# Weight low parts, convolution output and residual sums moved from POOL to DVE in a three-layer transformer kernel

## Chip, cores and metric

One core of one Trainium2 chip runs the whole program in one launch. The time is the device time in microseconds, the median of several runs. The core's engines are named as the profile names them: PE (TensorE, matrix products), PEld (its weight loads), DVE (VectorE), ACT (ScalarE), POOL (GpSimd), SP (SyncE, which issues the weight loads). Each engine works through its own instructions in order; work on different engines is ordered by semaphores alone. PEclk is the granted clock of TensorE, 1.00 for 2.4 GHz and 0.50 for 1.2 GHz.

## What is computed

512 tokens of 1024 features go through three layers, in float32.

```python
def hybrid_layer(x, c, positions, ...):             # layer 1
    ada = jax.nn.silu(c) @ w_ada + b_ada            # shift, scale and gate rows
    h = rms_norm(x, norm1_g) * (1 + scale1) + shift1
    proj = h @ w_in
    conv_out = bg * short_conv(cg * xc, conv_w)
    attn_out = dsa_attention(q, k, v, qi, ki, wi)   # 128 keys per query by an indexer
    mix = jnp.concatenate([conv_out, attn_out], axis=-1) @ w_out
    x = x + gate1 * mix
    h2 = rms_norm(x, norm2_g) * (1 + scale2) + shift2
    return x + gate2 * moe(h2, ...)                 # 64 experts, 8 a token, and a shared one

def expert_block(e, toks, gs):                      # in moe
    xb = t[toks]
    return ((silu(xb @ w1[e]) * (xb @ w3[e])) @ w2[e]) * gs[:, None]
```

Layers 2 and 3 are an attention with compressed keys (MLA) and a differential attention, each with a feed-forward block of width 2816 and layer norms. Their residual sums are `ALPHA * h + ...`.

## The kernel before

Every product is formed from two parts of its operands. An operand x is split into a high part of at most 12 significant bits (ACT, L217, `wh` for a weight tile) and the low part x minus high (a subtraction, L218, `wl`), and TensorE forms low x high, high x low and high x high (L225 to L227). `split` is the helper for all of them, so L217 and L218 stand for weights, transposed tokens (`xet`), transposed activations (`aet`) and others alike; the names tell them apart.

Weights come through `_Stream`: a list of tiles of up to 1 MB (128 partitions by 2048), loaded on SP's queue (L112) some tiles ahead into raw slots (`wraw`), then split. `get()` hands out a tile and, before that, emits the splits up to `ahead` tiles further on (`LA` = 2 in the experts). All raw tiles, high parts, low parts, transposed tokens and expert outputs (`eo`) share one pool of 22 slots of 8 KB per partition, the heap; a slot is written again only when its last reader is through, and where the reader is a transfer, when that has landed. Each tile of the list has a kind: `None` (not split), `True` (the low part is formed on DVE), or `"pool"` (the low part is formed on POOL). POOL has the convolution columns and output projection of layer 1 (`plan_attn`, `plan_sq`), the shared expert, the first two expert units and the w2 tile of all experts but the last (`plan_moe`), part of the MLA weights (`plan_mla`), some feed-forward tiles (`plan_ffn`) and most of the differential attention's input weights (`plan_diff`). POOL also forms the low part of the convolution output (`mixc`, L798), part of the residual sums of the attention half (`add` in `attn_block`, L846), and the adaptive rows (L657). It issues 51 gathers (L1213) and 67 scatters (L1218).

The expert half sorts tokens into slot blocks by expert. A unit of work is one of: 2 units of fixed experts, 25 single experts of one block, 3 experts of two blocks, and 16 pairs (two experts whose 64 rows each share a block). The order on each engine is that in which the program emits its work. For a single expert u it is:

- `get` of w1, which also emits the split of w2 of the unit before; products of w1 (`up`); `acts()` for the unit before: silu on ACT, times the w3 product on DVE (`sg`, L1395), transposes on TensorE (L230), their split (`aet`);
- `get` of w3, which emits the split of the next w1; products of w3; transposes of the next unit's gathered tokens (`xg`) and their split (`xet`, two pieces); the gather of a later block on POOL;
- `get` of w2 of the unit before, which emits the split of the next w3; its products (`down`), scaled to `eo` by DVE for the first half of the columns (L1414) and by ACT for the other (L1412); the scatter-add of `eo` to the sum `acc` in memory on POOL; the mask `P` of a later block (L1152) on DVE.

Where the slot tables of up to eight blocks are finished (a cut), DVE runs some ten small operations (L1134 to L1202), `gt` (L1140) among them. In the router, DVE finds the top 8 of 64 scores and packs the gates. In a pair, the two experts' products and down products alternate.

```python
kind = "pool" if i < 2 else True
j += [(weight("w1", 8, r), kind), (weight("w3", 8, r), kind)]
...
j.append((weight("w2", 2, r), "pool" if i < len(ops) - 4 else True))
```

Of the kernel before, what the change touches and what calls it, by code (L numbers as in the profile page):

```python
# [33 lines left out]
# slots of an expert by its rank: those below the first number have the second  # L34
# [36 lines left out]
class _Stream:  # L71
    """Weights in the order of use: loads run ahead on the SP queue, and each tile is split into two
    parts of at most 12 significant bits, whose sum is the float32 value, before it is used."""
# [41 lines left out]
    def _split(self):  # L115
        i = self.ns
        kind = self.jobs[i][1]
        if kind:
            t, n, v = self.rawt.pop(i)
            H, L = self.k.slot(F32R, "wh"), self.k.slot(F32R, "wl")  # L120
            self.k.split(H[:, :n], L[:, :n], t[:, :n], eng=self.k.nc.gpsimd if kind == "pool" else None)
            self.hl[i] = (H, L, n, v)
        self.ns += 1
# [7 lines left out]
    def more(self):  # L131
        """prepare one more tile than `ahead` asks for"""
        if self.ns < len(self.jobs):
            if self.ns not in self.rawt:
                self.pump(self.ns)
            self._split()
            self.pump(self.ns)
# [40 lines left out]
class _K:  # L178
# [35 lines left out]
    def split(self, H, L, x, scale=None, eng=None):  # L214
        nc = self.nc
        if scale is None:
            nc.scalar.activation(H, x, AF.Copy)  # L217
            (eng or nc.vector).tensor_tensor(out=L, in0=x, in1=H.bitcast(F32), op=OP.subtract)  # L218
# [13 lines left out]
    def rsqrt(self, v, n, scale, eps, name):  # L232
        """1 / sqrt(scale v + eps): a seed from the exponent, a third-order step and a Newton step, each on a
        multiple of the result that spares a product"""
# [50 lines left out]
    def proj(self, hT, nk, tiles, n=512, hook=None, w=None):  # L285
        """token-major product: weight tiles [p, kk, n] from chunk kc0 on into four PSUM tiles"""
# [33 lines left out]
    def part(self, hT, ps, tt, ws):  # L320
        """token tile tt of a product, weight tiles [(first chunk, tile)]"""
# [7 lines left out]
    def begin(self, xT):  # L329
        """the products of a block's first two weight tiles [128, 8, 256] with the first half of the tokens"""  # L330
# [16 lines left out]
    def begun(self, xT):  # L347
        """what `begin` has left of the next of its weight tiles"""
# [4 lines left out]
    def chunks(self, name, n):  # L353
        """feature-major operand in chunks of 128 features by 512 columns, as its two exact parts"""
# [39 lines left out]
    def plan_sq(self, w):  # L394
        w = w.rearrange("(k p) n -> p k n", p=128)
        return [(w[:, 4 * j:4 * j + 4, n * 512:n * 512 + 512], "pool") for j in range(2) for n in range(2)]

    def plan_attn(self):
# [3 lines left out]
        first += [(w, "pool") for w, _ in self.plan_win(2560)]  # L402
# [5 lines left out]
        j += [(cols[i:i + 2], "pool") for i in range(0, 12, 2)]  # L408
        out = self.plan_sq(self.a["w_out"][0])
        j += out[:2] + [(out[2][0], True)] + out[3:]  # L410
        return j

    def rope_p(self, t, cc, ss):
        """rotate the first 16 of each 64 columns of t [128, G, 64]; cc [128,16], ss [128,16] = [-sin | sin]"""
# [50 lines left out]
    def row(self, dst, ap, off, n):  # L465
        """one DRAM row on all partitions"""
        self.nc.scalar.dma_start(out=dst, in_=bass.AP(tensor=ap.tensor, offset=ap.offset + off, ap=[[0, 128], [1, n]]))

    def heads_T(self, dst, ps, g=None, scale=None):
        """four PSUM tiles [128 tok, 8 x 64]: (RMS norm with gain g,) partial rotation, feature-major split;  # L470
        the gain of the rotated columns goes in before the rotation, that of the others, in `scale`, after it"""
# [33 lines left out]
    def attn_block(self):  # L505
        nc, V, a, st = self.nc, self.nc.vector, self.a, self.st
        # adaptive scale and shift, and the normalised tokens, by halves of the features
# [86 lines left out]
        # remaining adaptive rows, on the scalar and Pool engines  # L594
# [68 lines left out]
        # indexer queries, keys, weights  # L663
# [43 lines left out]
        # indexer scores  # L707
# [31 lines left out]
        def topk():  # L739
            """the 128 best keys of each query, the earlier of equal ones: others get a bias of -1e30"""  # L740
# [23 lines left out]
        # values  # L764
# [5 lines left out]
        # short convolution, channel-major  # L770
# [5 lines left out]
        def conv():  # L776
            ws = []
            for c in range(4):
                w = lambda k: cw[:, k, c:c + 1]
                for i in range(3):  # L780
# [15 lines left out]
                    else:  # L796
                        V.tensor_tensor(out=y, in0=y, in1=ps, op=OP.mult)
                        self.split(*mixc(c), y, eng=nc.gpsimd)  # L798
# [8 lines left out]
        # attention  # L807
# [34 lines left out]
        def add(tt, ps, n):  # L842
# [3 lines left out]
            (V if n or last else nc.gpsimd).tensor_tensor(out=Y(tt)[:, c], in0=Y(tt)[:, c], in1=t, op=OP.add)  # L846
        last = False
        self.attend(range(HEADS), logits, value, fill(), FILL, 3)
        # the rest of the output projection and the residual, then the normalised tokens of the expert half
# [7 lines left out]
        def done(tt, *pss):  # L857
            nonlocal last
            last = tt == NT - 1
# [19 lines left out]
    def out_head(self, mix, add):  # L879
        """the first four chunks' share of an output projection; add(tt, ps, n) takes it in"""  # L880
# [22 lines left out]
    def pipeline(self, items, stages, fill=None, n=0, ready=None):  # L903
        """stages [(fn, delay)] over items; each step also emits up to n units of the background work `fill`,
        and as much of it as an item needs to be ready"""
# [24 lines left out]
    def attend(self, heads, logits, value, fill=None, n=0, bufs=3, ready=None):  # L930
        """softmax attention of `heads` in tiles of 128 queries, feature-major result"""
# [34 lines left out]
    def moe_units(self):  # L966
        """(ranks, rows of the slot blocks), in the order of work: the first FIX experts; the others by falling
        number of tokens, the busiest with two blocks, the least busy two to a block"""
# [20 lines left out]
    def plan_moe(self):  # L989
# [3 lines left out]
        j = [([wr, s1[:, :, 0:128]], "pool"), ([s1[:, :, 128:256], s3[:, :, 0:128]], "pool"),  # L993
             (s3[:, :, 128:256], "pool")]
# [13 lines left out]
        for i, (op, u, m) in enumerate(ops):  # L1008
            r = units[u][0][m]
            if op == "up":  # L1010
                kind = "pool" if i < 2 else True
                j += [(weight("w1", 8, r), kind), (weight("w3", 8, r), kind)]
                if i == 1:
                    j.append((kp(a["ws2"][0], 2), "pool"))
            else:
                j.append((weight("w2", 2, r), "pool" if i < len(ops) - 4 else True))
        return j

    def moe_begin(self, hT):
        """the router and most of the shared expert's first products, on the first half of the tokens"""  # L1020
# [66 lines left out]
    def moe_block(self, hT, h2d, x1d):  # L1087
# [20 lines left out]
        pos_b = self.const.tile([128, NT, NE], BF16, name="pos_b")  # exact up to 256, and above stays above  # L1108
# [10 lines left out]
        def pack(v, g, tmp):  # L1119
            """the gate in three exact parts"""  # L1120
# [8 lines left out]
        def tables(c, ig, is_):  # L1129
            """gather and scatter rows of n blocks from the sums c [128, n, 3] of token, tile base and one"""  # L1130
# [28 lines left out]
        def table_step(i):  # L1159
            """one block's slot list; the indices are finished for up to eight blocks at a time"""  # L1160
# [89 lines left out]
            # order of the experts  # L1250
# [40 lines left out]
            # gates  # L1291
# [31 lines left out]
        def shared():  # L1323
            """the rest of the shared expert, in steps"""
# [52 lines left out]
        # experts  # L1377
# [61 lines left out]
        def overflow():  # L1439
            """list of the blocks past the slots above"""  # L1440
# [103 lines left out]
        # blocks past the slots above  # L1544
# [63 lines left out]
    def moe_sum(self, X, acc, xT, xd):  # L1608
        """the layer's result, tile by tile: residual + gate2 * experts"""
# [536 lines left out]
```

## Time and profile before

| | us |
|---|---|
| runs | 2729.9, 2726.62, 2722.79 |
| median | 2726.62 |
| span of the profiled execution | 2724.9 |
| PE busy | 2361.5 (87%) |
| DVE busy | 1649.5 (61%) |
| ACT busy | 1056.4 (39%) |
| POOL busy | 836.8 (31%) |

The span is the stretch from the first to the last instruction that the profiler saw in one execution. A line of the page's groups gives the source line, the engine and operation, the tile written and the tiles read, their shapes, the count, the busy time, the mean of one in nanoseconds, and how long the engine sat idle just before such an instruction and what ended most of that. In the span, layer 1's attention half lies up to about 420 us, router and shared expert up to about 520, the experts up to about 1410, and layers 2 and 3 after that.

### The profile page before, as it was taken

Reading aid. Unit: us, or ns where it says so; the run is one execution under the profiler, and the core shown is the slowest. Engines: PE = TensorE matmul, PEld = TensorE weight load, DVE = VectorE, ACT = ScalarE, POOL = GpSimd, SP = SyncE. Lnnn points to the kernel's source line nnn. Section 1 sums busy time; section 2 is a strip of 40 time slices with the busy share of each in tenths; the row PEclk is TensorE's granted clock in tenths of the full one; section 3 lists DMA queues with packets and bytes.
Section 4 is the critical chain, followed back from the end, with each engine's and each line's share of the span. In section 5 each row is a group of like instructions: output and inputs, shape, how many; then the busy total and the mean of one; then the engine's idle time right before and its main releaser. Section 6 shows DMA issues by size and latency. Waiting matters only on the chain.

```text
span 2724.9 us, 33197 instructions
## 1 busy us (share of the span) xinstructions
PE 2361.5 (87%) x12964; PEld 1979.8 (73%) x12964; DVE 1649.5 (61%) x2445; ACT 1056.4 (39%) x1446; POOL 836.8 (31%) x308
## 2 busy tenths in 40 slices
PE   8778996778777887888758998999999998899998
PEld 4556765677666776777757877888888886788887
DVE  4699666577877877677656655333354666533234
ACT  2642433355545655555542532221313443222221
POOL 0653243456645655565521120000032221100001
PEclk9889998899988988898979999999999998999999
DMA  9432145588967877888861042223232122222321
GB/s 317 171 122 63 47 157 188 192 264 273 308 212 245 287 260 248 278 278 279 271 182 45 16 152 88 85 93 108 87 114 70 47 72 81 95 89 81 123 70 39
DMA packets 176593, 422.40 MB, mean 155 GB/s; under 512 B 19281, under 2 KB 97873, under 8 KB 151729
## 3 DMA queue, kind: packets, MB, share of 16 engines
q1 hardware_dynamic: 151552, 353.43, 37.8%
q0 software_dynamic: 12944, 39.20, 6.7%
q10 hardware_dynamic: 11938, 27.62, 2.8%
q8 instruction: 103, 1.69, 0.2%
q14 instruction: 56, 0.46, 0.1%
HBM read 390.78 MB, written 35.52 MB: 156 GB/s over the span
## 4 chain that ended last, share of the span: by engine, by line
PE 50%; DVE 22%; issue 9%; DMA 7%; ACT 6%; POOL 6%; ACTq 0%; POOLq 0%; DVEq 0%; SPq 0%
PE b L225 16%; PE b L226 15%; PE b L227 15%; DVE wl L218 5%; POOL wl L218 4%; ACT wh L217 4%; DMA acc<-eo,isc 3%; PE b L230 2%; DMA wraw<-in_w_dram 2%; DVE xet L218 1%; DVE gt L1140 1%; DVE work L752 1%; DVE eo L1414 1%; PE b L545 1%; POOL acc L1218 1%
## 5 line engine op out<-in xcount | busy, mean ns | idle before, releaser
L218 POOL TENSOR_TENSOR wl<-wraw,wh 128x2048 fp32r<-128x2048 f32 (+2 forms) x113 | 533.0, 4720 | 1208.6 <-ACT wh L217 1157.8
L218 DVE TENSOR_TENSOR wl<-wraw,wh 128x2048 fp32r<-128x2048 f32 x198 | 606.9, 3072 | 367.8 <-ACT wh L217 319.6
L217 ACT ACTIVATE wh<-wraw 128x2048 fp32r<-128x2048 f32 (+2 forms) x311 | 583.5, 1884 | 151.3 <-DVE wl L218 58.0
L225 PE MATMUL b<-xtl,wh 128*128 128x512 f32 (+1 forms) x928 | 342.5, 369 | 2.9 <-DVE xtl L218 2.9
L226 PE MATMUL b<-xth,wl 128*128 128x512 f32 (+1 forms) x928 | 341.0, 368 | 4.0 <-POOL wl L218 4.0
L227 PE MATMUL b<-xth,wh 128*128 128x512 f32 (+1 forms) x928 | 340.7, 367 | 0.0
L225 PE MATMUL b<-wl,xet 128*128 128x256 f32 x1072 | 319.2, 298 | 0.1
L226 PE MATMUL b<-wh,xet 128*128 128x256 f32 x1072 | 311.3, 290 | 0.8 <-DVE xet L218 0.8
L227 PE MATMUL b<-wh,xet 128*128 128x256 f32 x1072 | 310.8, 290 | 0.0
L1218 POOL DMA_INDIRECT acc<-eo,isc x67 | 102.6, 1531 | 391.9 <-DVE P L1152 121.6
L225 PEld LDWEIGHTS b<-wl,xet 128*128 128x128 f32 x1072 | 214.7, 200 | 1.7 <-ACT xet L217 0.2
L226 PEld LDWEIGHTS b<-wh,xet 128*128 128x128 f32 x1072 | 214.0, 200 | 2.4 <-DVE xet L218 0.9
L227 PEld LDWEIGHTS b<-wh,xet 128*128 128x128 f32 x1072 | 213.2, 199 | 0.0
L225 PE MATMUL b<-wl,aet 128*128 128x512 f32 x268 | 125.5, 468 | 99.6 <-POOL wl L218 99.1
L226 PEld LDWEIGHTS b<-xth,wl 128*128 128x128 f32 x928 | 175.0, 189 | 32.8 <-POOL wl L218 4.6
L225 PEld LDWEIGHTS b<-xtl,wh 128*128 128x128 f32 x928 | 175.0, 189 | 32.3 <-DVE xtl L218 3.6
L227 PEld LDWEIGHTS b<-xth,wh 128*128 128x128 f32 x928 | 174.9, 189 | 28.9
L225 PEld LDWEIGHTS b<-wl,aet 128*128 128x128 f32 x268 | 57.8, 216 | 121.2 <-POOL wl L218 108.8
L225 PE MATMUL b<-wl,ath 128*128 128x512 f32 x352 | 137.1, 390 | 0.0
L227 PE MATMUL b<-wh,ath 128*128 128x512 f32 x352 | 136.9, 389 | 0.0
L226 PE MATMUL b<-wh,atl 128*128 128x512 f32 x352 | 136.9, 389 | 0.0
L1213 POOL DMA_INDIRECT xg<-h2d,ig x51 | 124.6, 2444 | 34.3 <-issue 17.5
(463 smaller groups left out, 4649.8 us busy)
## 6 DMA issues: line engine op xcount, KB each, us to landing
wraw<-in_w_dram SPq DMA_DIRECT2D x192, 1024.0 KB
wraw<-in_ffn_w_gu_dram SPq DMA_DIRECT2D x44, 1024.0 KB
wraw<-in_w_ada_dram SPq DMA_DIRECT2D x24, 1024.0 KB
wraw<-in_ffn_w_down_dram SPq DMA_DIRECT2D x20, 1024.0 KB
wraw<-in_diff_w_in_dram SPq DMA_DIRECT2D x12, 1024.0 KB
wraw<-in_w_in_dram SPq DMA_DIRECT2D x8, 1024.0 KB
wraw<-in_w_in_dram SPq DMA_DIRECT2D x12, 512.0 KB
x<-in_x_dram SPq DMA_DIRECT2D x8, 512.0 KB
```

The costliest lines, as they stand in the source:

```text
L217: nc.scalar.activation(H, x, AF.Copy)
L218: (eng or nc.vector).tensor_tensor(out=L, in0=x, in1=H.bitcast(F32), op=OP.subtract)
L225: mm(ps, s[0], m[1], start=start, stop=False)
L226: mm(ps, s[1], m[0], start=False, stop=False)
L227: mm(ps, s[0], m[0], start=False, stop=stop)
L230: self.nc.tensor.transpose(ps, x, self.ident[:x.shape[0], :x.shape[0]])
L545: nc.tensor.matmul(ps, cb[:, kc, :], w[:, kk, :], start=False, stop=kc == 7)
L752: V.match_replace(work(qt), m8[qt - 1], work(qt), -3e38)
L1140: V.tensor_tensor(out=gt, in0=c[:, :, 2], in1=c[:, :, 1], op=OP.add)
L1213: nc.gpsimd.indirect_dma_start(out=x, out_offset=None, in_=h2d, in_offset=IndirectOffsetOnAxis(ap=idx, axis=0), bounds_check=S - 1, oob_is ...
L1218: nc.gpsimd.indirect_dma_start(out=acc, out_offset=IndirectOffsetOnAxis(ap=idx, axis=0), in_=o, in_offset=None, compute_op=OP.add)
L1414: V.tensor_scalar(o[rows, c], ps[rows], gate[rows], None, OP.mult)
```

## The change

The argument `eng` of `split` goes, and all kinds `"pool"` become `True`: 113 subtractions for weight low parts (105 of them 128 by 2048) run on DVE in their place of the program's order. So do the 4 low parts of the convolution output and the 7 residual sums. POOL keeps gathers, scatters, the adaptive rows and some fills. Comments and docstrings are left out too, so the changed program's lines have numbers up to five lower behind the changed places.

```diff
-            self.k.split(H[:, :n], L[:, :n], t[:, :n], eng=self.k.nc.gpsimd if kind == "pool" else None)
+            self.k.split(H[:, :n], L[:, :n], t[:, :n])
...
-    def split(self, H, L, x, scale=None, eng=None):
+    def split(self, H, L, x, scale=None):
...
-            (eng or nc.vector).tensor_tensor(out=L, in0=x, in1=H.bitcast(F32), op=OP.subtract)
+            nc.vector.tensor_tensor(out=L, in0=x, in1=H.bitcast(F32), op=OP.subtract)
...
-                        self.split(*mixc(c), y, eng=nc.gpsimd)
+                        self.split(*mixc(c), y)
...
-            (V if n or last else nc.gpsimd).tensor_tensor(out=Y(tt)[:, c], in0=Y(tt)[:, c], in1=t, op=OP.add)
+            V.tensor_tensor(out=Y(tt)[:, c], in0=Y(tt)[:, c], in1=t, op=OP.add)
...
-                kind = "pool" if i < 2 else True
-                j += [(weight("w1", 8, r), kind), (weight("w3", 8, r), kind)]
+                j += [(weight("w1", 8, r), True), (weight("w3", 8, r), True)]
...
-                j.append((weight("w2", 2, r), "pool" if i < len(ops) - 4 else True))
+                j.append((weight("w2", 2, r), True))
```

The other edits of this kind are in `plan_sq`, `plan_attn`, `plan_mla`, `plan_ffn` and `plan_diff`.

In a single expert's unit on DVE, before: the subtraction of w3, the scaled output, the next block's mask, then `sg`.

```order
L218 TENSOR_TENSOR wl<-wraw,wh 128x2048
L1414 TENSOR_SCALAR eo<-b,gt 128x512
L1152 TENSOR_TENSOR P<-iota_b,pos_b 128x4x64 x2
L1395 TENSOR_TENSOR sg<-sg,b 128x256
L218 TENSOR_TENSOR aet<-b,aet 128x256
L218 TENSOR_TENSOR wl<-wraw,wh 128x2048
L218 TENSOR_TENSOR xet<-b,xet 128x512 x2
L218 TENSOR_TENSOR wl<-wraw,wh 128x2048
```

The same place in the changed program:

```order
L218 TENSOR_TENSOR wl<-wraw,wh 128x2048
L1409 TENSOR_SCALAR eo<-b,gt 128x512
L1147 TENSOR_TENSOR P<-iota_b,pos_b 128x4x64 x2
L218 TENSOR_TENSOR wl<-wraw,wh 128x2048
L1390 TENSOR_TENSOR sg<-sg,b 128x256
L218 TENSOR_TENSOR aet<-b,aet 128x256
L218 TENSOR_TENSOR wl<-wraw,wh 128x2048
L218 TENSOR_TENSOR xet<-b,xet 128x512 x2
L218 TENSOR_TENSOR wl<-wraw,wh 128x2048
```

The subtraction of w2 stands between the mask `P` and `sg`; all else keeps its order.

On POOL, at the end of the first run of singles, before (`isc` holds the scatter's indices):

```order
L1218 DMA acc<-eo,isc 640x1024
L218 TENSOR_TENSOR wl<-wraw,wh 128x2048
L1213 DMA xg<-h2d,ig 64x1024
L1218 DMA acc<-eo,isc 640x1024
L218 TENSOR_TENSOR wl<-wraw,wh 128x2048
L1218 DMA acc<-eo,isc 640x1024
L1213 DMA xg<-h2d,ig 128x1024
L218 TENSOR_TENSOR wl<-wraw,wh 128x2048
L1218 DMA acc<-eo,isc 640x1024
```

and in the changed program:

```order
L1213 DMA acc<-eo,isc 640x1024
L1208 DMA xg<-h2d,ig 64x1024
L1213 DMA acc<-eo,isc 640x1024 x2
L1208 DMA xg<-h2d,ig 128x1024
L1213 DMA acc<-eo,isc 640x1024
```

A gather now follows the scatter ahead of it directly.

In the pairs on DVE, with the semaphores that each instruction waits for, before (DMASW are POOL's indirect transfers, DMAHW the loads, the others engines):

```order
L218 TENSOR_TENSOR aet<-b,aet 128x256 [waits Activation_49]
L218 TENSOR_TENSOR wl<-wraw,wh 128x2048 [waits DMAHW2_49,DVE_49,Activation_49]
L218 TENSOR_TENSOR wl<-wraw,wh 128x2048 [waits DMAHW3_49,PE_49,Activation_49]
L1414 TENSOR_SCALAR eo<-b,gt 64x512 [waits DMASW2_49,DMASW3_49,DMASW0_49,DMASW5_49,DVE_49,PE_49]
L1395 TENSOR_TENSOR sg<-sg,b 64x256 [waits Activation_49]
L218 TENSOR_TENSOR wl<-wraw,wh 128x2048 [waits DVE_49,DMAHW5_49,PE_49,Activation_49]
```

and in the changed program:

```order
L218 TENSOR_TENSOR wl<-wraw,wh 128x2048 [waits DMAHW4_49,Activation_49]
L1409 TENSOR_SCALAR eo<-b,gt 64x512 [waits PE_49]
L218 TENSOR_TENSOR wl<-wraw,wh 128x2048 [waits DMASW3_49,DMASW2_49,DMASW5_49,DMASW0_49,DMAHW5_49,DVE_49,Activation_49]
L1390 TENSOR_TENSOR sg<-sg,b 64x256 [waits Activation_49]
L218 TENSOR_TENSOR aet<-b,aet 128x256 [waits Activation_49]
L218 TENSOR_TENSOR wl<-wraw,wh 128x2048 [waits DMAHW6_49,DVE_49,Activation_49]
```

The wait for the indirect transfers, which stood at the scaled output `eo`, stands at the moved subtraction, ahead of `sg`; it is there in every second pair.

## Rows read from the trace of the kernel before

**Rows 1.** The page's costliest groups: count, busy us, mean ns of one, idle us before and releaser.
```profile
L218 POOL TENSOR_TENSOR wl<-wraw,wh 128x2048 fp32r<-128x2048 f32 (+2 forms) x113 | 533.0, 4720 | 1208.6 <-ACT wh L217 1157.8
L218 DVE TENSOR_TENSOR wl<-wraw,wh 128x2048 fp32r<-128x2048 f32 x198 | 606.9, 3072 | 367.8 <-ACT wh L217 319.6
...
L226 PE MATMUL b<-xth,wl 128*128 128x512 f32 (+1 forms) x928 | 341.0, 368 | 4.0 <-POOL wl L218 4.0
...
L225 PE MATMUL b<-wl,aet 128*128 128x512 f32 x268 | 125.5, 468 | 99.6 <-POOL wl L218 99.1
```

**Rows 2.** Timeline of DVE in one single expert: start us, duration us, operation.
```profile
894.57 2.28 DVE L218 TENSOR_TENSOR wl<-wraw,wh 128x2048 fp32r<-128x2048 f32 x1
896.77 0.74 DVE L1414 TENSOR_SCALAR eo<-b,gt 128x512 f32<-128x512 f32 x1
897.43 0.74 DVE L1152 TENSOR_TENSOR P<-iota_b,pos_b 128x256 bf16<-128x256 bf16 x2
898.10 0.41 DVE L1395 TENSOR_TENSOR sg<-sg,b 128x256 f32<-128x256 f32 x1
...
901.38 5.08 DVE L218 TENSOR_TENSOR wl<-wraw,wh 128x2048 fp32r<-128x2048 f32 x1 [1.38 <-ACT wh L217]
```

**Rows 3.** Timeline of POOL in the same expert.
```profile
899.24 5.07 POOL L218 TENSOR_TENSOR wl<-wraw,wh 128x2048 fp32r<-128x2048 f32 x1
904.47 2.94 POOL L1213 DMA_INDIRECT xg<-h2d,ig  x1 [0.16 <-issue]
```

**Rows 4.** Windows: length, busy us (count) of each engine, granted clock, DMA share, GB/s.
```profile
894.41:933.47 39.06, 31.47 (x240) 28.19 (x237) 31.70 (x28) 23.86 (x24) 26.92 (x9) 1.00 0.90 304
1087.16:1340.24 253.08, 209.04 (x1303) 187.79 (x1303) 187.77 (x111) 144.24 (x131) 146.01 (x49) 0.91 0.84 277
1198.60:1202.00 3.40, 3.14 (x7) 2.51 (x8) 3.40 (x2) 0.00 (x0) 0.21 (x1) 0.50 0.68 193
675.00:750.00 75.00, 58.71 (x434) 52.29 (x434) 62.48 (x57) 44.45 (x44) 50.40 (x19) 1.00 0.96 310
150.00:256.00 106.00, 79.18 (x345) 60.52 (x343) 101.42 (x223) 36.76 (x59) 49.85 (x26) 0.89 0.35 98
```

**Rows 5.** Timeline of PE in the same single expert; in brackets the idle time before.
```profile
898.65 0.47 PE L230 MATMUL b<-ident,sg 128*128 128x128 f32 x2 [1.07 <-DVE sg L1395]
898.88 0.36 PE L225 MATMUL b<-wl,xet 128*128 128x256 f32 x1
...
901.84 1.06 PE L230 MATMUL b<-ident,xg 128*128 128x128 f32 x8
904.36 0.50 PE L225 MATMUL b<-wl,aet 128*128 128x512 f32 x1 [1.46 <-POOL wl L218]
```

**Rows 6.** Timeline of ACT in the same expert.
```profile
902.49 1.09 ACT L217 ACTIVATE xet<-b 128x512 fp32r<-128x512 f32 x2 [1.14 <-PE b L230]
904.34 1.92 ACT L217 ACTIVATE wh<-wraw 128x2048 fp32r<-128x2048 f32 x1 [0.76 <-POOL wl L218]
```

**Rows 7.** Timeline of PE at the down products of a pair.
```profile
1198.86 0.80 PE L225 MATMUL b<-wl,aet 128*128 128x512 f32 x1 [3.03 <-POOL wl L218]
```

**Rows 8.** Timeline of DVE at a table cut.
```profile
865.67 5.33 DVE L1140 TENSOR_TENSOR gt<-tg 128x8 f32<-128x8 f32 x1
```

**Rows 9.** Timeline of PE behind that cut.
```profile
872.52 0.67 PE L230 MATMUL b<-ident,sg 128*128 128x128 f32 x2 [8.19 <-DVE sg L1395]
```

**Rows 10.** Timeline of DVE in the router, the first and the last of four.
```profile
435.64 4.67 DVE L1242 TENSOR_TENSOR ms<-ms,rb 128x256 f32<-128x256 f32 x1 [5.14 <-ACT ms L1241]
...
489.18 7.15 DVE L1152 TENSOR_TENSOR P<-iota_b,pos_b 128x512 bf16<-128x512 bf16 x4
```

**Rows 11.** Timeline of PE at the first expert unit's down products.
```profile
536.36 0.75 PE L225 MATMUL b<-wl,aet 128*128 128x512 f32 x1 [4.98 <-POOL wl L218]
```

**Rows 12.** Timeline of POOL at the table cut.
```profile
871.13 1.00 POOL L1213 DMA_INDIRECT xg<-h2d,ig  x1 [0.16 <-issue]
```

**Rows 13.** The chain that ended last, in order of time, in a pair: start, us, what.
```profile
1217.68 7.57 DMA acc<-eo,isc
```

More of the change, by code (lines that the diff above doesn't have):

```diff
@@ L395, in plan_sq @@
         w = w.rearrange("(k p) n -> p k n", p=128)
-        return [(w[:, 4 * j:4 * j + 4, n * 512:n * 512 + 512], "pool") for j in range(2) for n in range(2)]
+        return [(w[:, 4 * j:4 * j + 4, n * 512:n * 512 + 512], True) for j in range(2) for n in range(2)]
     def plan_attn(self):
@@ L401, in plan_attn @@
         first = head[1:] + self.plan_win(3584, 72) + self.plan_win(2048) + self.plan_win(1536)
-        first += [(w, "pool") for w, _ in self.plan_win(2560)]
+        first += self.plan_win(2560)
         rest = self.plan_ada([8, 9, 6, 7, 4, 5, 10, 11])
@@ L407, in plan_attn @@
         cols = [w[:, :, o + c * 128:o + c * 128 + 128] for c in range(4) for o in (0, 1024, 512)]
-        j += [(cols[i:i + 2], "pool") for i in range(0, 12, 2)]
+        j += [(cols[i:i + 2], True) for i in range(0, 12, 2)]
         out = self.plan_sq(self.a["w_out"][0])
-        j += out[:2] + [(out[2][0], True)] + out[3:]
-        return j
+        return j + out
     def rope_p(self, t, cc, ss):
@@ L845, in add @@
             V.tensor_tensor(out=t, in0=ps, in1=self.gate1[:, c], op=OP.mult)
-            (V if n or last else nc.gpsimd).tensor_tensor(out=Y(tt)[:, c], in0=Y(tt)[:, c], in1=t, op=OP.add)
-        last = False
+            V.tensor_tensor(out=Y(tt)[:, c], in0=Y(tt)[:, c], in1=t, op=OP.add)
         self.attend(range(HEADS), logits, value, fill(), FILL, 3)
@@ L857, in done @@
         def done(tt, *pss):
-            nonlocal last
-            last = tt == NT - 1
             for n in range(2):
@@ L992, in plan_moe @@
         wr, s1, s3 = kp(a["w_router"][0], 8), kp(a["ws1"][0], 8), kp(a["ws3"][0], 8)
-        j = [([wr, s1[:, :, 0:128]], "pool"), ([s1[:, :, 128:256], s3[:, :, 0:128]], "pool"),
-             (s3[:, :, 128:256], "pool")]
+        j = [([wr, s1[:, :, 0:128]], True), ([s1[:, :, 128:256], s3[:, :, 0:128]], True),
+             (s3[:, :, 128:256], True)]
         units = self.moe_units()
@@ L1010, in plan_moe @@
             if op == "up":
-                kind = "pool" if i < 2 else True
-                j += [(weight("w1", 8, r), kind), (weight("w3", 8, r), kind)]
+                j += [(weight("w1", 8, r), True), (weight("w3", 8, r), True)]
                 if i == 1:
-                    j.append((kp(a["ws2"][0], 2), "pool"))
+                    j.append((kp(a["ws2"][0], 2), True))
             else:
-                j.append((weight("w2", 2, r), "pool" if i < len(ops) - 4 else True))
+                j.append((weight("w2", 2, r), True))
         return j
@@ L1711, in plan_mla @@
             hs = slice(2 * i, 2 * i + 2)
-            j.append(([uq[:, :, hs, 0:128], uk[:, :, hs, :]], "pool"))
+            j.append(([uq[:, :, hs, 0:128], uk[:, :, hs, :]], True))
         return j + self.plan_sq(a["mla_w_o_2"][0])
@@ L1886, in plan_ffn @@
                 for o in (0, DFF):
-                    j.append((gu[:, :, o + f * 256:o + f * 256 + 256], "pool" if f == 0 else True))
+                    j.append((gu[:, :, o + f * 256:o + f * 256 + 256], True))
             for n in range(2):
                 for k in range(2 * f0, 2 * f1, 4):
-                    j.append((dn[:, k:min(k + 4, 2 * f1), n * 512:n * 512 + 512], "pool" if f0 and n else True))
+                    j.append((dn[:, k:min(k + 4, 2 * f1), n * 512:n * 512 + 512], True))
         return j
@@ L1949, in plan_diff @@
         w = self.a["diff_w_in_2"][0].rearrange("(k p) n -> p k n", p=128)
-        j = [(w[:, :, o + hp * 256:o + hp * 256 + 256], "pool" if hp or o < 2048 else True)
+        j = [(w[:, :, o + hp * 256:o + hp * 256 + 256], True)
              for hp in range(4) for o in (0, 1024, 2048)]
```

## The prediction

> **What bounds the kernel now.** I read the costliest groups first, then the timelines of the four engines over one expert, then windows by stage, then the chain of waits. TensorE is the engine to feed, and in the groups the question is who keeps it waiting: the down products (b from wl and aet) stood idle 99.6 us, 99.1 of it for POOL's low parts, while the 928 products on xth and wl, which are the projections of attention and of layers 2 and 3, stood 4.0 us for them [rows 1]. So what POOL's subtractions cost is in the expert half, and little elsewhere. The same groups show a second cost. One subtraction takes 4.72 us on POOL, and 3.07 us on DVE as a mean of 198. The timeline says why the mean is so high: the one at 894.57 took 2.28 us, with none running on POOL; the one at 901.38 took 5.08 us beside one on POOL that runs from 899.24 for 5.07 us, so to 904.31, and ended 2.15 us behind that [rows 2, 3]. DVE's subtraction stands still until POOL's is done. Over 198 of them that is 198 x (3.07 - 2.28) = 156 us of DVE time that is waiting.
>
> **A single expert.** Three of them take 39.06 us, 13.02 each, at a granted clock of 1.00 [rows 4]. TensorE has two holes in each: 1.07 us ahead of sg's transposes, for DVE, and 1.46 us ahead of the down products, for POOL [rows 5]. After the change the wait for POOL goes, but in DVE's order the w2 subtraction now stands between P and sg, and what is late next is sg. I add up the loop through it: wl 2.20 (894.57 to 896.77), eo 0.66, P 0.67, the moved wl 2.20, sg until the transposes start 0.55 (898.10 to 898.65) [rows 2, 5]; transposes 0.23, w3's products 2.96 (898.88 to 901.84), transposes of xg 0.65 until ScalarE starts on xet [rows 5, 6]; ScalarE's xet 1.09 and wh 1.92 [rows 6], and wl again. The sum is 13.1 us against 13.02 now. **Singles: nothing gained**, some 20 of them. DVE's subtraction there gets 2.8 us shorter and one of 2.2 us is put in. The two holes become one of about 2.5 us ahead of sg.
>
> **A pair** (two experts in one slot block). Ten take 253.08 us, 25.3 each, with a clock of 0.91 and a DMA share of 0.84 [rows 4]. A pair has one hole of 3.03 us for POOL's low part [rows 7], and 3.40 us at half clock behind it [rows 4]. The loop through the moved subtraction holds two of the pair's four up products more and a down product: 2.20 + 0.66 + 2.20 + 0.55 + 0.23, then four products of 2.96 (a down product is 12 matmuls of 512 columns where w3's is 24 of 256, so I take the same), 0.65 + 1.09 + 1.92 = 21.3 us. The DMA engines need no less: 0.84 x 25.3 = 21.3 us at a share of 1, and 22.1 us at the 0.96 that 675 to 750 reached [rows 4]. I take 22.1, a gain of 3.2, and 12 of the 16 pairs, since the first ones are mixed with table work: **-38 us**.
>
> **Table cuts.** Where the slot tables of up to eight blocks are finished, DVE's small gt stands 5.33 us behind POOL's subtraction [rows 8], and TensorE stands 8.19 us for sg [rows 9]. Without it gt, which has 8 columns, needs no more than sg's 0.41 [rows 2], and 2.2 us of moved wl come in: 5.33 - 0.41 - 2.2 = 2.7. Seven such places: **-19 us**. The clock behind the hole stays low, since 5 us of it are left.
>
> **Router.** Four DVE operations stand behind POOL there, from 4.67 us (ms) to 7.15 us (P, four of them) [rows 10], at about one POOL subtraction, 4.7 us [rows 1], each: -19. Four moved subtractions come into DVE's order, 4 x 2.2 = 9. **-10 us.**
>
> **First expert unit.** TensorE stands 4.98 us for a low part that is queued behind a scatter on POOL [rows 11]; on DVE it isn't behind it: **-5 us.**
>
> **Everything else.** The projections lose their 4.0 us: **-4 us.** In the indexer's top-k, 150 to 256, DVE is busy 101.4 of 106 us [rows 4]; five subtractions move there, which adds 5 x 2.2 = 11 us if DVE never stood for them on POOL, and takes off 5 x (4.7 - 2.2) = 12 if it stood for the whole of each: zero, with both as bounds. The 4 convolution and 7 residual operations lie beside TensorE work and cost nothing; uncovered they would cost 11 x 0.7 = 8. ScalarE's and SP's order doesn't change. What I cost at nothing on DVE is hidden by TensorE's products; in a single that cover is already used up.
>
> Sum: -38 - 19 - 10 - 5 - 4 = -76 on the profiled span of 2724.9, so 2648.9; the median of the runs is 1.7 above that span, which gives **2651 us**.
>
> **A rule and a row.** POOL's gather takes 2.94 us beside DVE's subtractions and 1.00 us when none runs [rows 3, 12], so each of the 118 gathers and scatters can become 1.94 us longer now that DVE subtracts more. I put nothing for it in the sum, since POOL has 533 us fewer to do [rows 1], but it lengthens the landing in rival C. The Trainium skill (SBUF — State Buffer, Who interferes with whom) says otherwise: a tensor_tensor of DVE leaves the descriptor writing of such DMAs alone, which the page marks as inferred. By the page rival C is priced at 7.57 us a wait, by the row at up to 9.5; the row decides here.
>
> **Rivals.**
> A. *DMA stays the bound in the pairs.* The DMA share there is 0.84, not 0.96, and the chain runs over a scatter that lands in 7.57 us [rows 13]: loads wait for slots, so the share can't rise. Then pairs give nothing: 2651 + 38 = **2689 us**. For it: the low clock stretch hides time in which loads caught up. Against: TensorE's hole there is ended by POOL, not by a load [rows 7].
> B. *The joined hole in the singles costs clock.* Now 1.07 and 1.46 us leave the clock at 1.00; behind 3.03 us it was at half for 3.40 us, so 1.7 us of work lost [rows 4, 5, 7]. A hole of 2.5 us lies between. If each of 20 singles pays: +34, **2685 us**.
> C. *Slower: DVE takes over POOL's waits for scatters.* A slot that a scatter reads is free only when it has landed. On POOL a subtraction stood behind that scatter in order anyway; on DVE it needs a wait of its own, and sg, aet and xet are queued behind. The order lists 19 DVE subtractions of weights with a wait for such a DMA, 11 before. If each of the 19 stands 7.57 us [rows 13]: 19 x 7.57 = 144, and 144 - 76 = +68, **2795 us**. It decides from 76 / 19 = 4.0 us each. Against: in the pairs only one of twelve subtractions has the mark, and six marked eo operations of before are one now, so of such waits on DVE there are 20 against 17. The new place is the worse one, ahead of sg.
> D. *The lock is not POOL's doing*, and DVE's subtractions stay at 3 us and more. Then 113 more on DVE are 113 x 3.07 = 347 us of it against 99 us of TensorE's waits that go; most of the 347 hides, so near no change, or slower. The rows speak against it: the end of the one follows the end of the other in the one shown [rows 2, 3].
>
> **How the numbers follow.** About 0.3%, 8 us, is what can be told from no change. The forecast has 0.55, its own range 2617 to 2682; A 0.14; B 0.15; C with D's worse part 0.11; what is left, 0.05, lies within 8 us of before. Faster: 0.55 + 0.14 + 0.15 = 0.84; same 0.05; slower 0.11. The low end takes the better bounds of each term: pairs at 21.3 (-10), the whole router (-3), singles 1 us better each (-20), the top-k's locks (-12): 2651 - 45 = 2606. The high end is A and B together, 2723, cut to 2716, since both at full price is unlikely; C lies outside.
>
> **What would show it.** Right: DVE's wl at 2.2 to 2.3 us throughout, and POOL with nothing but indirect DMAs and the adaptive rows after 400 us; gt at 0.17 us; pairs at 22 us and a DMA share near 0.96; one hole a single, ended by DVE's sg. A: pairs still at 25 us, holes ended by wh or by loads. B: singles at 14.5 us, clock under 1.00 between 675 and 750. C: DVE's wl with idle time ended by acc scatters. The prediction is wrong if singles move by more than 1 us either way, since there I claim that a 5 us wait and the 2.2 us put in its place cancel.

## Result and the profile after

The changed kernel takes 2660.0 us (median of 4 runs, 2654.9 to 2667.7) against 2728.3 before (4 runs, the three above among them): ratio 0.975, 95% interval 0.974 to 0.977. The forecast was 2651, range 2606 to 2716. The profiled execution has a span of 2660.0 us against 2724.9, so 64.9 us are to be found. Windows cut at the same instruction in both (ACT's `eo` of the second fixed expert, of the first pair and of the last unit) show where. The kernel before (length, busy time and count of PE, PEld, DVE, ACT, POOL, granted clock, DMA share, GB/s):

```profile
0.00:541.00 541.00, 433.97 (x2086) 326.50 (x2087) 379.74 (x750) 201.98 (x329) 205.06 (x106) 0.90 0.47 156
541.00:963.50 422.50, 331.29 (x2432) 299.23 (x2430) 326.94 (x342) 229.09 (x235) 251.35 (x87) 0.94 0.84 267
963.50:1407.90 444.40, 354.84 (x2226) 318.71 (x2225) 319.45 (x218) 240.69 (x222) 232.79 (x81) 0.90 0.80 260
1407.90:2724.90 1317.00, 1241.42 (x6228) 1035.36 (x6228) 623.35 (x1137) 384.64 (x660) 147.61 (x34) 0.97 0.25 83
```

and after:

```profile
0.00:526.10 526.10, 435.47 (x2087) 327.70 (x2088) 369.33 (x782) 201.82 (x330) 100.53 (x74) 0.91 0.48 161
526.10:954.00 427.90, 342.30 (x2431) 314.41 (x2429) 308.35 (x370) 226.93 (x236) 118.14 (x59) 0.91 0.87 264
954.00:1352.30 398.30, 344.29 (x2226) 318.57 (x2224) 295.70 (x249) 240.24 (x222) 110.10 (x50) 0.91 0.86 289
1352.30:2660.00 1307.70, 1235.27 (x6228) 1030.07 (x6228) 639.99 (x1171) 384.69 (x660) 1.40 (x1) 0.98 0.25 84
648.30:734.60 86.30, 69.52 (x472) 64.10 (x470) 60.54 (x57) 46.99 (x48) 27.16 (x12) 0.88 0.91 274
1077.40:1284.80 207.40, 182.46 (x1172) 170.55 (x1172) 156.56 (x118) 129.73 (x117) 58.66 (x26) 0.90 0.88 305
```

Four stages in each: up to that second unit -14.9 us, singles and table cuts +5.4, pairs -46.1, layers 2 and 3 -9.3. The last two rows of after are six singles (86.30 us, 14.4 each, clock 0.88; before 13.02 at 1.00 [rows 4]) and nine pairs (207.40 us, 23.0 each, clock 0.90; before 25.3 at 0.91 [rows 4]).

The page's groups of after:

```profile
L218 DVE TENSOR_TENSOR wl<-wraw,wh 128x2048 fp32r<-128x2048 f32 (+2 forms) x311 | 702.7, 2266 | 449.4 <-ACT wh L217 399.6
...
L226 PE MATMUL b<-xth,wl 128*128 128x512 f32 (+1 forms) x928 | 340.8, 367 | 0.0
...
L230 PE MATMUL b<-ident,sg 128*128 128x128 f32 x102 | 28.7, 377 | 132.9 <-DVE sg L1390 132.9
...
L225 PE MATMUL b<-wl,aet 128*128 128x512 f32 x268 | 113.4, 423 | 3.6 <-DVE wl L218 3.1
```

All 311 subtractions are on DVE and take 2.27 us as a mean; 198 took 3.07 and POOL's 113 took 4.72 [rows 1]. DVE's whole busy time is even lower, 1613.4 us against 1649.5, with 124 operations more. TensorE's wait for the low part of w2 fell from 99.1 us to 3.1. More than half of that came back elsewhere: the wait ahead of sg's transposes is 132.9 us, 52 more than in the kernel before:

```profile
L230 PE MATMUL b<-ident,sg 128*128 128x128 f32 x102 | 25.3, 336 | 80.9 <-DVE sg L1395 80.8
```

### The profile page after: what moved, and what is told of

It is laid out like the page before. It is cut to its first block, busy times and chain, and to the rows that moved or that the text cites. A ratio compares the mean times of both kernels' runs of the same rounds, so it can differ in the third digit from the quotient of the medians.

```text
span 2660.0 us, 32960 instructions
## 1 busy us (share of the span) xinstructions
PE 2357.3 (89%) x12964; PEld 1990.8 (75%) x12964; DVE 1613.4 (61%) x2569; ACT 1053.7 (40%) x1446; POOL 330.2 (12%) x184
## 4 chain that ended last, share of the span: by engine, by line
PE 61%; DVE 24%; ACT 8%; issue 3%; DMA 2%; POOL 1%; ACTq 0%; SPq 0%; DVEq 0%; POOLq 0%
PE b L225 19%; PE b L226 18%; PE b L227 18%; DVE wl L218 9%; ACT wh L217 4%; PE b L230 4%; ACT xet L217 2%; DVE eo L1409 1%; DVE P L1147 1%; PE b L544 1%; DVE work L751 1%; DVE m L747 1%; DMA wraw<-in_w_ada_dram 1%; DVE sg L1390 1%; DVE ln_st L1628 1%
## 5 line engine op out<-in xcount | busy, mean ns | idle before, releaser
L218 DVE TENSOR_TENSOR wl<-wraw,wh 128x2048 fp32r<-128x2048 f32 (+2 forms) x311 | 702.7, 2266 | 449.4 <-ACT wh L217 399.6
L225 PE MATMUL b<-wl,xet 128*128 128x256 f32 x1072 | 336.2, 314 | 0.1
L226 PE MATMUL b<-wh,xet 128*128 128x256 f32 x1072 | 327.0, 305 | 0.8 <-DVE xet L218 0.8
L227 PE MATMUL b<-wh,xet 128*128 128x256 f32 x1072 | 326.0, 304 | 0.0
L1213 POOL DMA_INDIRECT acc<-eo,isc x67 | 160.0, 2389 | 611.9 <-DVE P L1147 217.9
L226 PEld LDWEIGHTS b<-wh,xet 128*128 128x128 f32 x1072 | 230.9, 215 | 2.2 <-DVE xet L218 1.0
L225 PEld LDWEIGHTS b<-wl,xet 128*128 128x128 f32 x1072 | 231.0, 216 | 1.8 <-DVE wl L218 0.2
L227 PEld LDWEIGHTS b<-wh,xet 128*128 128x128 f32 x1072 | 229.8, 214 | 0.0
L230 PE MATMUL b<-ident,sg 128*128 128x128 f32 x102 | 28.7, 377 | 132.9 <-DVE sg L1390 132.9
L923 ACT ACTIVATE p<-b,nm 128x128 f32<-128x128 f32 (+3 forms) x128 | 67.1, 526 | 166.5 <-DVE nm L920 127.2
L230 PEld LDWEIGHTS b<-ident,sg 128*128 128x128 f32 x102 | 16.0, 206 | 141.9 <-issue 92.0
L225 PE MATMUL b<-wl,aet 128*128 128x512 f32 x268 | 113.4, 423 | 3.6 <-DVE wl L218 3.1
```

Of the source, the lines that this page charges most:

```text
L218: nc.vector.tensor_tensor(out=L, in0=x, in1=H.bitcast(F32), op=OP.subtract)
L225: mm(ps, s[0], m[1], start=start, stop=False)
L226: mm(ps, s[1], m[0], start=False, stop=False)
L227: mm(ps, s[0], m[0], start=False, stop=stop)
L230: self.nc.tensor.transpose(ps, x, self.ident[:x.shape[0], :x.shape[0]])
L923: nc.scalar.activation(p[:, :nk], ps[:, :nk], AF.Exp, bias=nm, accum_out=sm)
```

## Experiments

The theory: DVE's subtraction, and other DVE operations that read two operands from the local memory (`gt`, the mask `P`), stand still while POOL's subtraction runs, and the change takes that away. In the singles it gives the gain back, since w2's subtraction ahead of sg makes one long hole where two short ones were, and TensorE's clock falls behind it. Rivals: DVE was stretched by waits, not by POOL; the gain lies in other parts than w2; the singles are held by DMA.

### POOL busy with work nobody needs

Behind the scatters of each down product in the changed kernel, four subtractions of 512 columns, from a constant tile (`db`) into a spare one:

```diff
+                for _ in range(4):
+                    nc.gpsimd.tensor_tensor(out=dout.rearrange("p (a b) -> p a b", b=128), in0=db, in1=db, op=OP.subtract)
```

> The changed kernel, and behind each scatter POOL does four subtractions of 512 columns from a constant tile into a spare one; nothing reads them, so nobody waits for their result. Theory (DVE's subtraction stands still while POOL's runs): DVE's weight subtractions go up from a mean of 2.27 us to 2.6 or more, and the time by 15 to 50 us. Rival (DVE was stretched by what it waited for, not by POOL's use of memory): mean 2.27 us, time within 4 us of 2660.

Measured: 2725.5 us (10 runs), ratio to before 0.999 (0.998 to 1.001). Nothing reads what POOL writes, and 65 us are lost, more than the 15 to 50 that I wrote. The mean of DVE's 128x2048 subtractions rose from 2.295 to 2.442 us, less than I wrote: POOL's pieces let DVE in between, as the first rows show, where gt and P end while POOL's four are still running. A table cut of this run, DVE, POOL and PE in turn:

```profile
873.83 1.88 DVE L1135 TENSOR_TENSOR gt<-tg 128x8 f32<-128x8 f32 x1
...
875.83 2.45 DVE L1147 TENSOR_TENSOR P<-iota_b,pos_b 128x256 bf16<-128x256 bf16 x2
878.20 3.12 DVE L218 TENSOR_TENSOR wl<-wraw,wh 128x2048 fp32r<-128x2048 f32 x1
```

```profile
874.13 5.04 POOL L1544 TENSOR_TENSOR dout<-dum 128x512 bf16<-128x512 f32 x4
```

```profile
881.92 0.67 PE L230 MATMUL b<-ident,sg 128*128 128x128 f32 x2 [8.98 <-DVE sg L1390]
```

gt takes 1.88 us, P 2.45 and the subtraction 3.12 while POOL's four run, and TensorE's hole is 8.98 us, longer even than before the change (8.19 [rows 9]). In the changed kernel, without POOL's work, the same place reads (DVE, then PE):

```profile
854.89 0.17 DVE L1135 TENSOR_TENSOR gt<-tg 128x8 f32<-128x8 f32 x1
...
855.17 0.75 DVE L1147 TENSOR_TENSOR P<-iota_b,pos_b 128x256 bf16<-128x256 bf16 x2
855.84 2.29 DVE L218 TENSOR_TENSOR wl<-wraw,wh 128x2048 fp32r<-128x2048 f32 x1
```

```profile
858.73 0.67 PE L230 MATMUL b<-ident,sg 128*128 128x128 f32 x2 [4.76 <-DVE sg L1390]
```

The stages of the idle run, singles and cuts, then pairs (after the change 427.9 and 398.3):

```profile
525.70:983.30 457.60, 354.03 (x2434) 326.39 (x2431) 333.72 (x370) 226.79 (x235) 298.53 (x171) 0.87 0.80 248
983.30:1408.80 425.50, 345.42 (x2226) 319.35 (x2225) 331.71 (x249) 240.27 (x222) 357.30 (x182) 0.90 0.80 270
```

### POOL busy without reading

In the same place, 15 fills of a spare tile of 384 columns:

```diff
+                for _ in range(15):
+                    nc.gpsimd.memset(dout, 1.0)
```

> As the run with idle subtractions on POOL, but POOL fills a spare tile instead (15 fills of 384 columns behind each scatter, some 5 us), so it writes and reads nothing. Theory (DVE stands for POOL's reading, not for POOL being busy or for scatters and gathers being late): DVE's weight subtractions stay at a mean of 2.3 us, gt at 0.17 us, and the time within 10 us of 2660. Rival (late gathers and scatters behind POOL's work cost the time): about 2725 us as with the idle subtractions.

Measured: 2685.7 us, ratio 0.984 (0.982 to 0.986). The groups by form, DVE's subtraction and POOL's fills:

```profile
L218 DVE TENSOR_TENSOR wl<-wraw,wh 128x2048 fp32r<-128x2048 f32 x298 | 682.4, 2295 | 442.7 <-ACT wh L217 385.3 <-PE b L225 27.2 <-issue 15.6
```

```profile
L1541 POOL MEMSET dout<- 128x384 f32 x960 | 435.6, 454 | 51.6
```

The same table cut, POOL and then DVE:

```profile
853.49 7.61 POOL L1541 MEMSET dout<- 128x384 f32 x15
```

```profile
853.50 0.75 DVE L1147 TENSOR_TENSOR P<-iota_b,pos_b 128x256 bf16<-128x256 bf16 x2
854.17 2.28 DVE L218 TENSOR_TENSOR wl<-wraw,wh 128x2048 fp32r<-128x2048 f32 x1
```

POOL is as busy (436 us; the idle subtractions were 463) and DVE is not stretched: P takes 0.75 us and the subtraction 2.28 beside the fills, and the mean is 2.295 us as in the changed kernel. (gt, at 853.21, ends before the fills begin, so its 0.17 us here shows nothing.) So it is POOL's reading that holds DVE, not its being busy. But 26 us are lost all the same, where the theory claimed at most 10. Its stages (singles and cuts, pairs, the rest):

```profile
524.20:952.30 428.10, 342.49 (x2431) 314.59 (x2428) 308.36 (x370) 227.07 (x236) 307.07 (x480) 0.91 0.85 265
952.30:1361.10 408.80, 354.02 (x2226) 328.16 (x2224) 296.23 (x249) 240.15 (x222) 309.07 (x541) 0.88 0.85 281
1361.10:2682.10 1321.00, 1234.98 (x6228) 1030.65 (x6228) 640.22 (x1171) 384.52 (x660) 16.92 (x36) 0.97 0.25 83
```

Singles and cuts take what they took after the change (428.1 against 427.9 us). The pairs take 10.5 us more with a hole as long and a lower clock, and behind the experts TensorE waits up to 28.6 us for DVE's sums, 13.5 after the change: the last scatters stand behind the last fills. So reading on POOL is worth the 30 us that the run above has more in singles and cuts. In the pairs it isn't so plain. The stage read 387.1 us in `w2_only` and 404.3 in `mask_late` (both below), which have the changed kernel's order there, so 10.5 us is little more than that spread. And ten pairs without table work take 237.6 us with idle subtractions and 238.9 with fills, against 230.2 after the change and 253.0 before: what reading costs more shows in the table cuts. There the theory is at its clearest. The five units in which gt was stretched took 107.7 us before, 83.8 after the change, 108.0 with idle subtractions and 85.4 with fills.

### Which part of the change

In the kernel before, only the w2 tiles moved (`w2_only`); in the changed kernel, only they moved back (`all_but_w2`):

```diff
-                j.append((weight("w2", 2, r), "pool" if i < len(ops) - 4 else True))
+                j.append((weight("w2", 2, r), True))
```

> The kernel before with only the experts' w2 subtractions moved to DVE; router, shared expert, first two units, convolution, output projection, later layers and the residual sums as before on POOL. Theory: the stretch up to the first unit and layers 2 and 3 keep their time of before, which was 14.9 and 9.3 us more, and the experts gain as in the change: 2660 + 24 = 2684 us. Rival (the gain in the experts comes from other slots and loads, not from w2): 2700 us and more.

> The changed kernel with only the experts' w2 subtractions back on POOL; all else stays on DVE. Theory (the parts add): the 15 us ahead of the first unit and the 9 us in layers 2 and 3 are kept, the experts lose their gain of about 41 us: about 2702 us, singles at 13.0 us with two holes, pairs at 25 us, gt at 5 us in the cuts. Rival (the gain sits in the other parts): 2670 us.

Measured, in this order: 2670.2 us, ratio 0.978 (0.975 to 0.982), and 2717.8 us, ratio 0.995 (0.993 to 0.997). By the medians -59.5 and -12.8 us, together -72.3 against the change's -68.3: within the noise the parts add, and w2 is some five sixths of it. I had given the other parts 24 us; they are 13. With w2 back on POOL the expert stages are those of before (426.0 and 444.2 us against 422.5 and 444.4), so what changed there is w2. In the first stage the cuts of the two runs read 534.5 and 533.2 (526.1 after, 541.0 before), so each has about half of its 15. In layers 2 and 3 no gain can be told: the changed kernel took 1307.7 us there and `w2_after_sg`, with the same code in that stretch, 1320.8; before it was 1317.0. So the -9.3 of the stages above lies within that spread.

### Where w2's subtraction stands

In the changed kernel, the tile that is split at `get` of w1 has its rounding on ACT at once, and its subtraction on DVE (`flush`) behind sg, ahead of `aet`:

```diff
-            self.k.split(H[:, :n], L[:, :n], t[:, :n])
+            if self.held is not None and i == self.ng + 1:
+                self.k.nc.scalar.activation(H[:, :n], t[:, :n], AF.Copy)
+                self.held.append((H[:, :n], L[:, :n], t[:, :n]))
...
                     act(sg, ps, rows)
+                flush()
```

> The changed kernel, but DVE's subtraction for w2 is emitted behind sg instead of ahead of it; ScalarE's rounding stays where it was. Theory (the moved subtraction ahead of sg makes one hole of 2.8 us in TensorE per expert, and behind it half the clock): the hole and the low clock go; the loop through sg is then 2.20 + 0.66 + 0.67 + 0.55 + 0.23 + 2.96 + 0.65 + 1.09 + 1.92 = 10.9 us, so singles fall from 13.1 to 14.4 us each to what the loads need, about 12.2 us, and pairs lose a hole of 2.8 us: 2660 - 20 x 2.0 - 12 x 1 = about 2608 us. Rival 1 (DMA holds singles at 13 us): only the low clock goes, about 2636 us. Rival 2 (the down products then wait for the later w2 part): the hole only changes its place, 2660 us.

Measured: 2612.4 us, ratio 0.957 (0.955 to 0.958). The hole ahead of sg's transposes in the singles of this run, and of the changed kernel:

```profile
855.03 0.48 PE L235 MATMUL b<-ident,sg 128*128 128x128 f32 x2 [0.65 <-DVE sg L1395]
...
865.89 0.48 PE L235 MATMUL b<-ident,sg 128*128 128x128 f32 x2 [0.65 <-DVE sg L1395]
```

```profile
901.09 0.67 PE L230 MATMUL b<-ident,sg 128*128 128x128 f32 x2 [2.85 <-DVE sg L1390]
```

0.65 us against 2.85, and a single here takes 10.9 us (855.03 to 865.89) against 14.3: the loop that I had added up as 10.9. The DMA share over two such singles is 1.01, and they aren't held at 13 or at 12 by it:

```profile
851.20:873.00 21.80, 20.51 (x165) 18.70 (x162) 19.69 (x20) 15.72 (x17) 6.14 (x4) 1.00 1.01 349
```

But not all run so. Six other singles take 13.9 us each; in one of them DVE's subtraction stands 5.61 us for a load:

```profile
623.30:706.60 83.30, 64.81 (x456) 59.41 (x455) 60.10 (x56) 47.05 (x49) 19.09 (x13) 0.90 0.94 293
668.23 2.29 DVE L223 TENSOR_TENSOR wl<-wraw,wh 128x2048 fp32r<-128x2048 f32 x1 [5.61 <-DMA wraw<-in_w_dram]
```

Over the stage the time from one `eo` to the next, table cuts and the units behind a two-block expert left out, is 12.7 us in the mean, against 14.0 after the change. So the move is worth 1.3 us a unit, and rival 1 (loads) holds in part of them.

### The mask

```diff
-                for i in range(nt[0], min(nt[0] + 2, ng[0] + 12, NB)):
-                    if i not in masks:
-                        table_mask(i)
                 w = st.get()
...
                 acts()
+                for i in range(nt[0], min(nt[0] + 2, ng[0] + 12, NB)):
+                    if i not in masks:
+                        table_mask(i)
                 w = st.get()
```

Once with w2 where the change has it, once with w2 behind sg:

> The changed kernel, with the mask P of a later block made behind aet instead of ahead of the moved subtraction; w2's subtraction stays ahead of sg. It takes 0.67 us out of the loop of a single and so shortens TensorE's hole there from 2.85 to about 2.2 us; pairs have no mask in the loop and stay. Theory (the hole's length costs twice, as idle time and by the low clock behind it): 25 x 0.67 = 17 us of idle time, and less of the low clock behind the holes, up to 1.1 us a single more: 2620 to 2643 us. Rival (the low clock comes whatever the hole's length): 2643 us and singles as often at half clock as before.

> As the run with w2 behind sg, and the mask P of a later block is made behind aet as well. Theory: once w2 is behind sg the loop through sg (10.9 us) no longer binds, so taking 0.67 us more out of it changes nothing: within 4 us of the run with w2 alone. Rival: DVE's path to sg still binds, then 25 singles x 0.67 = 17 us less.

Measured: 2661.1 us, ratio 0.973 (0.969 to 0.977), the same as the change, where the theory said 2643 or less; and 2594.0 us, ratio 0.949 (0.947 to 0.952). Six singles in each run, `mask_late` first:

```profile
646.70:729.80 83.10, 70.09 (x476) 64.66 (x473) 60.79 (x57) 47.02 (x48) 23.42 (x12) 0.88 0.93 294
```

```profile
634.30:697.00 62.70, 61.31 (x474) 55.91 (x471) 59.62 (x57) 47.09 (x49) 23.56 (x11) 1.00 0.97 306
```

In the first, TensorE's hole fell from 2.85 to 2.16 us as planned:

```profile
652.04 0.47 PE L230 MATMUL b<-ident,sg 128*128 128x128 f32 x2 [2.16 <-DVE sg L1390]
...
665.92 0.48 PE L230 MATMUL b<-ident,sg 128*128 128x128 f32 x2 [2.16 <-DVE sg L1390]
```

Still the time stayed. The starts are 13.88 us apart, single after single, where the sum without a lower clock is 13.07 - 0.69 = 12.4 (the hole got 0.69 us shorter); six take 83.1 us at a clock of 0.88, the changed kernel's 86.3 at the same. Over all singles and cuts it is 425.0 against 427.9. In the changed kernel the clock stayed up in some singles, and those took 13.07 us (1.00 over 882.0 to 895.1, below), which is the 13.1 of my sum:

```profile
882.00:895.10 13.10, 10.25 (x86) 9.35 (x84) 10.10 (x11) 7.84 (x8) 4.50 (x2) 1.00 0.96 299
895.10:909.40 14.30, 11.45 (x84) 10.55 (x81) 10.15 (x11) 7.84 (x8) 4.48 (x2) 0.88 0.92 288
```

In the second run the holes are all but gone, the clock is 1.00, and a single takes 10.45 us, nearly all of it TensorE's own work (61.31 of 62.70 us). There my theory was wrong: with w2 behind sg DVE's path to sg still bound, and a single that waits for nothing else went from 10.86 to 10.45 us. If each of the 27 singles gains that, it is 11 us of the 18 between the medians. But the long waits went too at this place (six singles took 83.3 us in the run above, 62.7 here), others came elsewhere, and no run tells apart what the mask and what their new places are worth.

### What holds the pairs then

In the kernel of the last run (2594 us) the next wait is the one of rival C. Its waits for landing scatters (us in total, times, longest):

```profile
POOL acc L1218 <- DMA acc<-eo,isc: 58.8, 10, 10.0
...
ACT eo L1412 <- DMA acc<-eo,isc: 29.8, 5, 9.3
```

A slot comes round for the next `eo` before the scatter that reads it has landed, and ACT waits up to 9.3 us; four of its five waits lie in the pairs, and every fourth pair takes some 8 us more than the others, not the 15 that I wrote below. Two changes of how far ahead loads run, both made to that kernel:

```diff
-LR=8; LA=2; MOE_RAW=7
+LR=7; LA=2; MOE_RAW=7
```

> The run with w2 behind sg and the mask late, with loads 7 instead of 8 tiles ahead in the experts. That run (2594 us) loses some 15 us in every fourth pair where eo waits up to 9 us for an earlier scatter to land in its slot. Theory (a raw tile held less gives slots earlier): some 2585 us. Rival (the slots come round in turn, so fewer raw tiles only delay the loads): 2594 us or more.

Measured: 2595.4 us, ratio 0.952 (0.950 to 0.953): no gain as a whole, since the pairs' stage fell from 377.8 to 356.0 us while the singles got holes of the same kind (their stage rose from 379.3 to 389.0, the one before it from 521.6 to 529.1). So, 8 ahead for the singles and 7 for the pairs:

```diff
+            if len(ranks) > 1 and st.raw == LR:
+                st.raw = 7
```

> The run with w2 behind sg and the mask late, loading 8 tiles ahead up to the first pair and 7 in the pairs. With 8 throughout the singles took 10.45 us each and the pairs waited for landing scatters every fourth time; with 7 throughout it was the other way round (singles with holes, the stretch of pairs 22 us shorter). Theory (how far ahead loads go decides which slot meets an unlanded scatter, stage by stage): both gains together, about 2575 us. Rival (the slots' turn as the pairs begin decides, not the number): the pairs keep their holes, 2590 us or more.

Measured: **2573.3 us, ratio 0.943 (0.942 to 0.945)**, the fastest of the study. Nine pairs:

```profile
1005.60:1194.60 189.00, 170.45 (x1172) 157.31 (x1171) 155.22 (x117) 129.89 (x117) 67.69 (x27) 0.96 0.95 340
```

21.0 us each at a clock of 0.96 and a DMA share of 0.95, against 23.0 at 0.90 in the changed kernel. Two of the nine still have a hole of 5 to 6 us.

## Why the prediction held, and where it was off

The direction and the size held: -68 us by the medians against -76 forecast. The lock, the router and the first unit held as mechanisms. The step on the singles failed, by the prediction's own sign: they moved by more than 1 us each. That the sum came so near is in part luck, since misses cancel. The time between ACT's `eo` of one block and of the next, added up by kind of unit, gives the whole 64.9 us of the profiled executions (there are 27 single experts, two of them behind the pairs):

| stretch, in us | before | after | measured | forecast |
|---|---|---|---|---|
| router and first units, with all ahead of them | 541.0 | 526.1 | -14.9 | -15 |
| five units with a table cut | 107.7 | 83.8 | -24.0 | -19 |
| three units behind a two-block expert | 56.0 | 38.2 | -17.8 | no term |
| the other 25 intervals of the singles' stage | 322.4 | 350.9 | +28.5 | 0 |
| the pairs, and two late singles | 380.8 | 353.4 | -27.4 | -38 |
| layers 2 and 3 | 1317.0 | 1307.7 | -9.3 | -4 |

- *The lock.* The premise, read from one subtraction that ended 2.15 us behind POOL's [rows 2, 3], is confirmed by the two runs with idle POOL work: reading on POOL stretches DVE, writing alone doesn't.
- *Router and first unit*, -10 and -5: at the first `eo` the changed kernel is 10.9 us ahead, at the second, where the wait of 4.98 us stood [rows 11], another 4.0. With only w2 moved it is 1.9 and 4.6, with all but w2 7.7 and 0.1, so the first term belongs to the other parts of the change and the second to w2.
- *Table cuts*, 2.7 us each in seven places: the trace of before has nine gt, and five of them are stretched (5.3 to 5.6 us). These gave 4.8 each. At the cut shown the hole fell from 8.19 [rows 9] to 4.76 us, gt from 5.33 [rows 8] to 0.17.
- *Units behind a two-block expert* had no term. POOL's subtraction began behind a scatter there, and TensorE stood for it:

```profile
649.72 0.79 PE L225 MATMUL b<-wl,aet 128*128 128x512 f32 x1 [6.68 <-POOL wl L218]
```

- *Singles*, nothing gained: this step failed, in the way of rival B. The loop was right, 13.07 us where the clock stays up, but the joined hole costs clock in most of them: the six of the first table took 14.4 us each against 13.02. I had B at 0.15 and 1.7 us each; it came, at 1.4 us.
- *Pairs*, -38: the loop of 21.3 us was right, and the 22.1 that I took for DMA's sake was not what held them. In the changed kernel a pair is one part of 9.45 us and one that depends on the clock, behind the same hole of 2.77 us:

```profile
1077.43:1089.23 11.80, 9.03 (x64) 8.28 (x63) 9.32 (x7) 6.97 (x7) 2.90 (x1) 1.00 0.78 273
1142.68:1155.99 13.31, 10.54 (x64) 9.76 (x63) 10.83 (x8) 6.96 (x7) 2.90 (x1) 0.87 1.02 365
1213.17:1227.61 14.44, 11.67 (x64) 10.87 (x63) 11.11 (x8) 6.96 (x7) 2.84 (x1) 0.76 0.77 258
```

At full clock that is 9.45 + 11.80 = 21.25 us. The ten pairs of [rows 4] came down from 253.0 to 230.2 us, 2.3 each and not 3.2, as the clock is 0.90 over them. In `w2_only`, with the same order in the pairs, it is 0.96, and they take 22.0 us each:

```profile
1066.84:1286.90 220.06, 192.27 (x1302) 179.39 (x1301) 173.55 (x131) 144.07 (x131) 62.72 (x30) 0.96 0.92 320
```

- *Projections of layers 2 and 3*, -4: their wait for POOL went from 4.0 us to nothing, but the stage tells nothing, by the spread of 13 us between runs of the same code.
- *Rival A* (DMA) fell: with other waits gone the share went to 0.95 and 0.97.
- *Rival C* (waits for scatters): in the changed kernel DVE's subtractions waited for a landing scatter once, 2.8 us, not 19 times. The marks in the order told where such a wait may come, not that it does. It came when the units got faster, and then it was worth 21 us (2594 to 2573).

## What to carry to other kernels

POOL's subtractions cost DVE time even where nobody waited for their result (gt 5.33 us against 0.17): look for operations whose duration jumps while the neighbour runs, and add up the jump before calling work on the neighbour free. When work moves to an engine in program order, ask what it now stands ahead of: here the same operation two places later was worth another 48 us (2660 to 2612) beside the 68 of the move. And a hole in TensorE can have a price in clock besides its length: two holes of 1.07 and 1.46 us cost nothing of it, one of 2.2 us cost 1.5 us a single, and one of 2.77 us in a pair nothing, 1.5 or 2.6 us. And a sum that comes out right is no proof of its terms: add up the trace by kind of unit and compare term by term.

## What was not expected of the hardware

A hole of 2.16 us was followed by the same loss in one single after another in `mask_late`, while behind 2.85 us (the changed kernel) some singles stayed at full clock, and behind 2.77 us some pairs; the longer hole wasn't the dearer one. These runs don't say why.

POOL's gathers and scatters are stretched by DVE's subtractions, as one row had shown ahead of the change. In the changed kernel, POOL, and DVE's subtraction beside the second scatter:

```profile
854.22 1.44 POOL L1213 DMA_INDIRECT acc<-eo,isc  x1 [8.32 <-DVE isc L1132]
855.96 3.05 POOL L1208 DMA_INDIRECT xg<-h2d,ig  x1 [0.30 <-issue]
...
898.49 3.44 POOL L1213 DMA_INDIRECT acc<-eo,isc  x1 [8.27 <-DVE P L1147]
902.23 1.04 POOL L1208 DMA_INDIRECT xg<-h2d,ig  x1 [0.30 <-issue]
```

```profile
898.32 2.29 DVE L218 TENSOR_TENSOR wl<-wraw,wh 128x2048 fp32r<-128x2048 f32 x1
```

The gather beside the subtraction at 855.84 takes 3.05 us, one without a subtraction of a weight beside it 1.04; the scatter beside the subtraction at 898.32 takes 3.44 us, the one at 854.22, ahead of a subtraction, 1.44. The Trainium skill (SBUF — State Buffer, Who interferes with whom) has the exclusive lock, and that a DVE instruction with two inputs in that memory contends with a GpSimd instruction that reads it, not with one that only writes it; both runs with idle POOL work agree (P and the subtraction took 2.45 and 3.12 us beside reading, 0.75 and 2.28 beside writing). It also infers that descriptor writing isn't held by DVE's tensor_tensor. The rows here show that the whole instruction on POOL is held, by 2 us. A gather or scatter also reads its indices (`ig`, `isc`), and no run tells whether that reading or the writing of descriptors was held, so the inference stands open.
